# The first norms of an encoder trunk: x loaded ahead of the identity, operand parts written straight from PSUM, weights set behind the norms

## The chip, the cores and the metric

The kernel runs on one core of one Trainium2 chip. The core has TensorE (matrix products, into the accumulation memory PSUM with its 8 banks), VectorE, ScalarE (ACT), GpSimd (POOL) and SyncE (SP, which here only issues transfers), and 16 DMA engines that all transfers share. The metric is the device time of one execution in microseconds (us); of the kernel before there are three runs, 2758.95, 2759.03 and 2759.92 us, with the median 2759.03.

## The reference, cut to what matters

Two sequences, of 512 and 256 tokens of width 1024, go through the same two layers. A layer is: a gated feed-forward network (FFN), a token mixer, and a second FFN, each on normed input and added to x. Layer 0 mixes by a gated linear recurrence in both directions, layer 1 by windowed attention; a last norm closes the trunk. All is in 32-bit floats.

```python
def rmsnorm(x, g):
    y = xf * lax.rsqrt(jnp.mean(xf * xf, axis=-1, keepdims=True) + NORM_EPS)
    return (y * g.astype(F32)).astype(x.dtype)

def swiglu_ffn(x, w1, w2):                       # w1: 1024 x 5632, w2: 2816 x 1024
    gate, up = jnp.split(x @ w1, 2, axis=-1)
    return (jax.nn.silu(gate) * up) @ w2

for li in range(DEPTH):                          # DEPTH = 2
    x = x + 0.5 * swiglu_ffn(rmsnorm(x, norm_g[li, 0]), ffn_w1[li, 0], ffn_w2[li, 0])
    ...
```

## The kernel before

The 768 tokens of both sequences are six blocks of 128 rows; blocks 0 to 2 are half 0 and blocks 3 to 5 half 1, so a half has 384 columns once it is turned. x stays in on-chip memory (SBUF).

*Products.* A product of two 32-bit operands is made of three products of a faster, shorter format (fp32r): each operand is split into a high part, which is the operand rounded by a copy, and a low part, the operand less the high part. `mm3` gives high x high, high x low and low x high, where the weight is the first factor in `up_plain`: its low part is wanted by the third product, the low part of the activations by the second. ACT makes high parts and VectorE low parts.

*Start.* `setup` loads the identity (SP's queue) and the norm scales, lower bounds and head scales (ACT's queue), turns the latter on TensorE and copies them into `cols`. `load_x` issues, on SP, blocks 0 to 2 of x, the first two weight tiles, then blocks 3 to 5; later weights follow. At most four raw weight tiles are held, so the fifth waits until the first was split. `norm_block` squares and sums a block on ACT, takes the root on ACT, inverts it on VectorE and scales the block there. `turn(half, part, row)` turns four of the eight 128-column slices of a half on TensorE, three transposes to a bank; ACT copies each bank, times the norm's scale, into a plain block (`tn`), and `put` splits two slices at a time into operand parts: a cast on ACT and a subtraction on VectorE over 768 elements. Norms and turns of half 1 are put into a list (`later`), and `up_plain` takes one entry at set places between its products (`run_later`).

*FFN.* The first two column tiles of the gate and of the up half of `w1` are done by plain products (`up_plain`): for each half of the tokens four weight tiles, eight slices of 1024 each, three products a slice; 192 products of 384 columns in all. Its end for one tile is Silu on ACT and a multiplication on VectorE. The other 20 column tiles are done in pairs (`up_pair`, `product`, L423) by a scheme of seven block products in place of eight, which needs sums and differences of the four operand blocks: `sums` makes them on VectorE from the plain blocks `tn` and splits them (`t1`, `t4`, `t3`, `t2`, for two slices at a time). A pair takes its seven products in the order of `UP`: first `p1` with the block b00, then `p7` with `t3`. `down_quad` does the same for `w2`; ahead of its first group six additions and subtractions on VectorE (L483, L484) bring x into the form that the scheme wants.

*What sets the order.* The program is written in one order, and a planner sets each engine's order before the run from its own estimate of costs: an instruction that is ready by that estimate may go ahead of an earlier one that is not. So the six additions of L483 and L484 run on VectorE between 13 and 31 us, and the load of the sinks (L121) is ACT's first issue. `issue_after(ins)` holds what is traced in its block behind `ins`, on the engine of `ins` alone; it adds no wait. In the kernel before it keeps the loads in order and the first norms one behind the other.

## Time and profile before

| | |
|---|---|
| median of three runs | 2759.03 us |
| profiled execution, its own time | 2760.57 us |
| its span, from the first to the last instruction | 2758.8 us |
| mean granted clock of TensorE | 0.998 |
| TensorE products, busy | 2733.7 us (99%), 17281 |
| VectorE busy | 2100.5 us (76%) |
| ACT busy | 1327.5 us (48%) |
| POOL busy | 309.2 us (11%) |
| first product of `up_plain` | at 14.78 us |
| first product of L423 | at 54.80 us |

How to read the lines below. A line of the timeline has the start in us from the span's start, the time to the end of the last of the group, the engine, the line of the kernel, the operation, the tiles written and read with their shapes, and the number of instructions merged; in brackets stands the idle time of the engine just before and what ended it. SPq and ACTq are issues of transfers, PEld the load of the fixed operand of a product. Products overlap, so the time from one start to the next (the pitch) is shorter than one's duration; fp32r products appear as f32. A line of the table of windows has the window, its length, the busy time and the number of instructions of each engine asked for (all of them in the order TensorE, weight load, VectorE, ACT, POOL), the granted clock of TensorE as a share of full speed, the DMA engines' share and GB/s. A line of groups has the line, the engine, the operation, the tiles and shapes, the count, then the busy time in us and the mean of one in ns, then idle time before.

### The profile page before, as it was taken

How to read it: one execution, taken by the hardware profiler on the slowest of the kernel's cores; microseconds unless marked ns; L12 is line 12 of the kernel's file. 1: busy time of each engine (PE TensorE's matmuls, PEld its weight loads, DVE VectorE, ACT ScalarE, POOL GpSimd, SP SyncE). 2: the span in 40 equal slices, each digit the busy share in tenths (PEclk: the TensorE clock that was granted, in tenths of full speed). 3: DMA queues.
4: the chain of work that ended last, by engine and by line, in shares of the span. 5: the costliest groups of instructions: out<-in, count | busy, mean ns of one | idle time of the engine just before them, and what ended most of it. 6: DMA issues, size and time to landing. Idle time of an engine off the chain costs nothing.

```text
span 2758.8 us, 44483 instructions
## 1 busy us (share of the span) xinstructions
PE 2733.7 (99%) x17281; PEld 2481.9 (90%) x17281; DVE 2100.5 (76%) x3662; ACT 1327.5 (48%) x2479; POOL 309.2 (11%) x315
## 2 busy tenths in 40 slices
...
DMA packets 330117, 291.63 MB, mean 106 GB/s; under 512 B 11609, under 2 KB 257841, under 8 KB 329905
## 3 DMA queue, kind: packets, MB, share of 16 engines
...
## 4 chain that ended last, share of the span: by engine, by line
PE 95%; DVE 2%; ACT 2%; DMA 1%; issue 0%; DVEq 0%; SPq 0%; ACTq 0%
PE ps L423 41%; PE ps L498 20%; PE ps L263 9%; PE ps L265 9%; PE ps L264 9%; PE ps L694 1%; PE ps L1230 1%; PE ps L1169 1%; PE ps L839 1%; PE ps L1221 1%; PE ps L325 1%; DMA wr<-wr 1%; PE ps L815 0%; DVE x L520 0%; ACT big L328 0%
## 5 line engine op out<-in xcount | busy, mean ns | idle before, releaser
L423 PE MATMUL ps<-big,w 128*128 128x384 f32 x6720 | 1169.2, 334 | 0.0
L423 PEld LDWEIGHTS ps<-big,w 128*128 128x128 f32 x6720 | 1165.9, 188 | 1.6
L204 ACT CAST w<-wr 128x512 fp32r<-128x512 f32 x600 | 415.1, 706 | 707.4 <-DVE wr L218 371.6
L205 DVE TENSOR_TENSOR w<-wr,w 128x512 fp32r<-128x512 f32 (+1 forms) x520 | 448.5, 866 | 180.9 <-ACT w L204 176.0
L498 PE MATMUL ps<-w,big 128*128 128x512 f32 x2520 | 579.0, 390 | 2.0 <-DVE x L520 1.9
L498 PEld LDWEIGHTS ps<-w,big 128*128 128x128 f32 x2520 | 471.0, 188 | 104.8 <-ACT big L268 4.5
L520 DVE SCALAR_TENSOR_TENSOR x<-ps,x 128x512 f32<-128x512 f32 x468 | 303.6, 683 | 10.2 <-PE ps L265 10.0
L146 POOL DMA_DIRECT2D s<-wr x120 | 105.1, 875 | 1662.9 <-DMA wr<-in_ffn_w_dram 804.5
L263 PE MATMUL ps<-w,big 128*128 128x512 f32 x624 | 253.0, 405 | 0.3
L265 PE MATMUL ps<-w,big 128*128 128x512 f32 x624 | 244.8, 392 | 1.0 <-DVE big L332 1.0
L264 PE MATMUL ps<-w,big 128*128 128x512 f32 x624 | 244.8, 392 | 0.0
L268 ACT CAST big<-tA 128x384 fp32r<-128x384 f32 x296 | 148.1, 513 | 162.2 <-DVE tA L458 76.8
L263 PE MATMUL ps<-big,w 128*128 128x384 f32 (+2 forms) x640 | 219.2, 344 | 3.2 <-ACT big L268 1.9
L264 PE MATMUL ps<-big,w 128*128 128x384 f32 (+2 forms) x640 | 216.3, 338 | 0.7 <-DVE big L269 0.6
L265 PE MATMUL ps<-big,w 128*128 128x384 f32 (+2 forms) x640 | 215.5, 337 | 0.0
L269 DVE TENSOR_TENSOR big<-tA,big 128x384 fp32r<-128x384 f32 x296 | 183.9, 632 | 12.9 <-ACT big L268 12.0
L172 DVE TENSOR_TENSOR w<-wr,w 128x1024 fp32r<-128x1024 f32 x92 | 111.9, 1222 | 78.4 <-ACT w L171 72.6
L263 PEld LDWEIGHTS ps<-w,big 128*128 128x128 f32 x624 | 117.5, 188 | 29.3 <-issue 5.6
L205 POOL TENSOR_TENSOR w<-wr,w 128x512 fp32r<-128x512 f32 x80 | 123.3, 1541 | 179.7 <-ACT w L204 155.2
L171 ACT CAST w<-wr 128x1024 fp32r<-128x1024 f32 x92 | 96.5, 1052 | 97.3 <-PE ps L264 77.7
L265 PEld LDWEIGHTS ps<-w,big 128*128 128x128 f32 x624 | 117.4, 188 | 27.7 <-DVE big L332 1.7
L264 PEld LDWEIGHTS ps<-w,big 128*128 128x128 f32 x624 | 117.7, 189 | 21.8 <-issue 0.4
...
## 6 DMA issues: line engine op xcount, KB each, us to landing
wr<-in_ffn_w_dram SPq DMA_DIRECT2D x264, 512.0 KB, 3.9
...
```

Of the source, the lines that this page charges most:

```text
L146: self.nc.gpsimd.dma_start(out, src, accum_op=ALU.add)
L172: self.nc.vector.tensor_sub(lo, raw, hi.bitcast(F32))
L204: nc.scalar.copy(h, src)
L205: low = (eng or nc.vector).tensor_sub(l, src, h.bitcast(F32)).ins
L263: nc.tensor.matmul(out, a[0], b[0], start=first, stop=False)
L264: nc.tensor.matmul(out, a[0], b[1], start=False, stop=False)
L265: nc.tensor.matmul(out, a[1], b[0], start=False, stop=last)
L268: self.nc.scalar.copy(hi, src)
L269: self.nc.vector.tensor_sub(lo, src, hi.bitcast(F32))
L423: self.nc.tensor.matmul(ps, a[x], b[y], start=first and k == 0 and i == 0, stop=k == 3 and i == 2, skip_group_check=True,)
L498: nc.tensor.matmul(ps, a[x], w[y], start=name == chain and kp == 0 and q == 0, stop=kp == 1 and q == 2, skip_group_check=True,)
L520: self.nc.vector.scalar_tensor_tensor(x, ps, c, x, ALU.mult, ALU.add)
```

## The change

- `setup`: VectorE first clears a tile, and TensorE does 21 products of that tile with itself (128 x 128, into a bank that nobody reads). The identity is loaded from ACT's queue and not from SP's. The turning of the scales is put off into a function, `turn_cols`, whose copy stands behind the scaling of block 2 on VectorE.
- `norm_block`: block 1's square and sum run on VectorE (`tensor_tensor_reduce`).
- `turn(..., straight=True)` for half 0: from each bank ACT writes the high part and VectorE the low part of the operand; the plain blocks that `sums` needs are put together there, high plus low, by four additions of 768 elements.
- The first weight's subtraction is done in two halves of 512.
- Order: the first weight is staged between the two turns of half 0, the second after them; the norms of half 1 follow in `load_x` itself and no longer out of the list, the third weight behind the scaling of block 4 and the fourth behind that of block 5; the sinks' load stands behind the last root, Silu behind it too; the four additions in `sums` and the six of `down_quad` stand behind the scaling of block 5 or, once it is there, the last low part of b01. In the list two empty entries take the first two places, so that the turns of half 1 and the sums are taken one place later.

```diff
@@ -41,6 +41,7 @@
 RAWBUFS = 4
 SLOTS = 21
 RING = 1024
+WARM = 21
 UP = ("p1", "p7", "p2", "p5", "p4", "p6", "p3")
 DOWN = ("p1", "p2", "p5", "p4", "p7", "p6", "p3")
 FACTOR = {"p1": "b00", "p2": "b10", "p3": "b11", "p4": "t4", "p5": "t1", "p6": "t2", "p7": "t3"}
@@ -94,12 +95,17 @@
         nc, cp = self.nc, self.cp
         self.consts = consts
         ident, rows = consts[0], consts[4]
+        zero = self.tmp(TA)[:, :P]
+        nc.vector.memset(zero, 0.0)
         self.eps = cp.tile([P, 1], F32, name="eps")
         nc.vector.memset(self.eps, EPS)
+        idle = self.ps(P)
+        for _ in range(WARM):
+            nc.tensor.matmul(idle, zero, zero, start=True, stop=True)
+        raw = self.tmp(P)
+        nc.scalar.dma_start(raw, ident)
         warm = self.stat(1)
         nc.scalar.activation(warm, self.eps, AF.Sqrt)
-        raw = self.tmp(P)
-        nc.sync.dma_start(raw, ident)
         self.identr = cp.tile([P, P], F32R, name="ident_r")
         nc.vector.tensor_copy(self.identr, raw)
         self.ident = self.identr.bitcast(F32)
@@ -109,10 +115,14 @@
         for r in rows:
             nc.scalar.dma_start(cols[lo : lo + r.shape[0], :], r)
             lo += r.shape[0]
-        pt = self.ps(n)
-        nc.tensor.transpose(pt, cols[:n, :], self.ident[:n, :n])
         self.cols = cp.tile([P, n], F32, name="cols")
-        nc.vector.tensor_copy(self.cols, pt)
+
+        def turn():
+            pt = self.ps(n)
+            nc.tensor.transpose(pt, cols[:n, :], self.ident[:n, :n])
+            nc.vector.tensor_copy(self.cols, pt)
+
+        self.turn_cols = turn
 
     def load_tables(self):
         nc, cp = self.nc, self.cp
@@ -169,7 +179,10 @@
             n = shape[0] * shape[1]
             hi, lo = (self.wtile()[:, :n].rearrange("p (a b) -> p a b", a=shape[0]) for _ in range(2))
             self.nc.scalar.copy(hi, raw)
-            self.nc.vector.tensor_sub(lo, raw, hi.bitcast(F32))
+            some = shape[0] if self.staged else NC // 2
+            for k in range(0, shape[0], some):
+                ks = slice(k, k + some)
+                self.nc.vector.tensor_sub(lo[:, ks, :], raw[:, ks, :], hi[:, ks, :].bitcast(F32))
             self.staged[key] = (hi, lo, 2)
 
         return [(2, go)]
@@ -266,11 +279,12 @@
 
     def split(self, src, hi, lo):
         self.nc.scalar.copy(hi, src)
-        self.nc.vector.tensor_sub(lo, src, hi.bitcast(F32))
+        return self.nc.vector.tensor_sub(lo, src, hi.bitcast(F32)).ins
 
     def load_x(self, srcs):
         nc = self.nc
         self.x = [None] * NBLK
+        self.whole = []
         last = None
         blocks = [srcs[s][lo : lo + P, :] for s, (_, n) in enumerate(SEQS) for lo in range(0, n, P)]
         for b, src in enumerate(blocks):
@@ -285,31 +299,39 @@
         order = None
         for b in range(HB):
             with self.tc.issue_after(order) if order else nullcontext():
-                order = self.norm_block(b)
-        self.turn(0, 0, 0)
-        self.turn(0, 1, 0)
+                order = self.norm_block(b, b == 1)
+        with self.tc.issue_after(self.scaled):
+            self.turn_cols()
+        self.turn(0, 0, 0, True)
         with self.tc.issue_after(order):
             self.stage_next()
-            self.stage_next()
-        self.load_tables()
-
-        def rest():
-            for b in range(HB, NBLK):
-                self.norm_block(b)
-
-        self.later(rest, lambda: self.turn(1, 0, 0), lambda: self.turn(1, 1, 0), self.sums)
-
-    def norm_block(self, b):
+        self.turn(0, 1, 0, True)
+        self.stage_next()
+        for b in range(HB, NBLK):
+            with self.tc.issue_after(order):
+                order = self.norm_block(b)
+            if b > HB:
+                with self.tc.issue_after(self.scaled):
+                    self.stage_next()
+        self.normed, self.mixed = order, self.scaled
+        with self.tc.issue_after(order):
+            self.load_tables()
+        self.later(lambda: None, lambda: None, lambda: self.turn(1, 0, 0), lambda: self.turn(1, 1, 0), self.sums)
+
+    def norm_block(self, b, on_dve=False):
         nc = self.nc
         xn, r = self.big([P, D]), self.stat(1)
-        nc.scalar.activation(xn, self.x[b], AF.Square, accum_out=r)
+        if on_dve:
+            nc.vector.tensor_tensor_reduce(xn, self.x[b], self.x[b], 1.0, 0.0, ALU.mult, ALU.add, r)
+        else:
+            nc.scalar.activation(xn, self.x[b], AF.Square, accum_out=r)
         last = nc.scalar.activation(r, r, AF.Sqrt, bias=self.eps, scale=1.0 / D).ins
         nc.vector.reciprocal(r, r)
-        nc.vector.tensor_scalar(xn, self.x[b], r, None, ALU.mult)
+        self.scaled = nc.vector.tensor_scalar(xn, self.x[b], r, None, ALU.mult).ins
         self.xn[b] = xn
         return last
 
-    def turn(self, half, part, row):
+    def turn(self, half, part, row, straight=False):
         nc = self.nc
         feeds_ffn = row % 3 != 1
         if half == 0 and part == 0:
@@ -324,15 +346,28 @@
                 src = self.xn[HB * half + i][:, m * P : (m + 1) * P]
                 nc.tensor.transpose(pt[:, i * P : (i + 1) * P], src, self.ident)
             g = self.cols[:, row * NC + m : row * NC + m + 1]
-            if feeds_ffn:
+            if straight:
+                key = (f"b{part}{half}", m % 4 // 2)
+                if key not in self.ops:
+                    self.ops[key] = self.big([P, 2, 2, H], F32R)
+                hi, lo = (self.ops[key][:, m % 2, i, :] for i in range(2))
+            elif feeds_ffn:
                 nc.scalar.activation(self.block(part, half, m % 4), pt, AF.Copy, scale=g)
                 continue
-            hi, lo = (self.h[m][:, i, half * H : (half + 1) * H] for i in range(2))
+            else:
+                hi, lo = (self.h[m][:, i, half * H : (half + 1) * H] for i in range(2))
             nc.scalar.activation(hi, pt, AF.Copy, scale=g)
             nc.vector.scalar_tensor_tensor(lo, pt, g, hi.bitcast(F32), ALU.mult, ALU.subtract)
-        if feeds_ffn:
-            for kp in range(2):
-                self.put(f"b{part}{half}", kp, self.tn[(part, half)][:, kp])
+        for kp in range(2 if feeds_ffn else 0):
+            name = f"b{part}{half}"
+            if straight:
+                self.block(part, half, 0)
+                hi, lo = (self.ops[(name, kp)][:, :, i, :].bitcast(F32) for i in range(2))
+                self.whole.append((self.tn[(part, half)][:, kp], hi, lo))
+            else:
+                low = self.put(name, kp, self.tn[(part, half)][:, kp])
+                if self.mixed and part == 0:
+                    self.mixed = low
 
     def block(self, part, half, k):
         if (part, half) not in self.tn:
@@ -341,7 +376,7 @@
 
     def put(self, name, kp, src):
         t = self.ops[(name, kp)] = self.big([P, 2, 2, H], F32R)
-        self.split(src, t[:, :, 0, :], t[:, :, 1, :])
+        return self.split(src, t[:, :, 0, :], t[:, :, 1, :])
 
     def operand(self, name, k):
         t = self.ops[(name, k // 2)]
@@ -359,11 +394,16 @@
         put("t2", b11)
 
     def sums(self):
+        with self.tc.issue_after(self.mixed) if self.whole else nullcontext():
+            for parts in self.whole:
+                self.nc.vector.tensor_add(*parts)
+        self.whole = []
         for kp in range(2):
             tiles = (self.tn[(i // 2, i % 2)][:, kp] for i in range(4))
             self.mix(*tiles, lambda name, src: self.put(name, kp, src))
 
     xn = [None] * NBLK
+    normed = mixed = None
 
     def after_block(self, b, row):
         if row is None:
@@ -411,7 +451,9 @@
                 self.done((tag, j, c))
             pss.append(ps)
         t = self.tmp(H)
-        self.nc.scalar.activation(t, pss[0], AF.Silu)
+        with self.tc.issue_after(self.normed) if self.normed else nullcontext():
+            self.nc.scalar.activation(t, pss[0], AF.Silu)
+        self.normed = None
         self.nc.vector.tensor_mul(t, t, pss[1])
         return t
 
@@ -480,8 +522,10 @@
         if g == 0:
             for i in range(HB):
                 x12, x21, x22 = cols(HB + i, 0), cols(i, 1), cols(HB + i, 1)
-                nc.vector.tensor_add(x12, x12, x22)
-                nc.vector.tensor_sub(x21, x21, x22)
+                with self.tc.issue_after(self.mixed) if self.mixed else nullcontext():
+                    nc.vector.tensor_add(x12, x12, x22)
+                    nc.vector.tensor_sub(x21, x21, x22)
+            self.mixed = None
         banks = {}
         for name in DOWN:
             wh, wl = self.take((tag, "down", g, name))
```

## The prediction

> **What bounds the kernel now.** I read the page first, for the bound of the whole, then the timeline of the first 60 us, where everything in the change lies, then the table of windows for the clock and for VectorE's load.
>
> ```profile
> span 2758.8 us, 44483 instructions
> PE 2733.7 (99%) x17281; PEld 2481.9 (90%) x17281; DVE 2100.5 (76%) x3662; ACT 1327.5 (48%) x2479; POOL 309.2 (11%) x315
> ```
>
> TensorE is busy for 99% of the span, so at most some 25 us (2758.8 - 2733.7) can be had from idle time, and what is to be had at the start is the time until the stream of products runs without a stop. The timeline shows how that time goes:
>
> ```profile
> 0.74 0.38 SPq L102 DMA_DIRECT2D tB<-in_ident_dram  x1
> 1.18 1.37 SPq L279 DMA_DIRECT2D x<-in_x_prompt_dram  x3
> 5.57 1.06 ACT L305 ACTIVATE big<-x 128x1024 f32<-128x1024 f32 x1 [2.88 <-DMA x<-in_x_prompt_dram]
> 8.09 4.75 PE L325 MATMUL ps<-ident_r,big 128*128 128x128 f32 x24 [0.42 <-DVE big L308]
> 10.07 0.75 DVE L308 TENSOR_SCALAR big<-x,stat 128x1024 f32<-128x1024 f32 x1
> 10.15 1.05 ACT L171 CAST w<-wr 128x1024 fp32r<-128x1024 f32 x1 [0.31 <-DMA wr<-in_ffn_w_dram]
> 11.23 1.22 DVE L172 TENSOR_TENSOR w<-wr,w 128x1024 fp32r<-128x1024 f32 x1 [0.41 <-ACT w L171]
> 12.02 2.00 ACT L328 ACTIVATE big<-ps,cols 128x384 f32<-128x384 f32 x4 [0.82 <-PE ps L325]
> 13.88 1.58 ACT L268 CAST big<-big 128x768 fp32r<-128x768 f32 x2
> 14.76 1.83 DVE L269 TENSOR_TENSOR big<-big,big 128x768 fp32r<-128x768 f32 x2 [0.89 <-ACT big L268]
> 14.78 0.44 PE L263 MATMUL ps<-big,w 128*128 128x384 f32 x1 [1.95 <-ACT big L268]
> 15.78 0.69 PE L264 MATMUL ps<-big,w 128*128 128x384 f32 x1 [0.55 <-DVE big L269]
> ...
> 21.28 0.33 PE L263 MATMUL ps<-big,w 128*128 128x384 f32 x1
> 24.92 1.03 PE L325 MATMUL ps<-ident_r,big 128*128 128x128 f32 x8
> 26.14 0.34 PE L265 MATMUL ps<-big,w 128*128 128x384 f32 x1
> 26.57 1.98 ACT L171 CAST w<-wr 128x1024 fp32r<-128x1024 f32 x2
> 27.65 0.44 PE L263 MATMUL ps<-big,w 128*128 128x384 f32 x1 [1.17 <-ACT w L171]
> 27.92 2.35 DVE L172 TENSOR_TENSOR w<-wr,w 128x1024 fp32r<-128x1024 f32 x2
> 28.47 0.42 PE L264 MATMUL ps<-big,w 128*128 128x384 f32 x1
> 29.19 0.45 PE L265 MATMUL ps<-big,w 128*128 128x384 f32 x1
> ```
>
> The first of the 192 products of `up_plain` starts at 14.78, the second at 15.78. The first weight's 24 products end where the second weight's begin, at 21.28. The third weight is cast late (26.57), so TensorE waits at 27.65 and again for the low part at 29.19. After that nothing stops it until the pair products of L423:
>
> ```profile
> 54.80 5.36 PE L423 MATMUL ps<-big,w 128*128 128x384 f32 x30
> ```
>
> (5.36 - 0.33) / 29 = 0.173 us is the pitch of one product at full clock. 192 of them are 33.3 us, and the 24 transposes of the second half, at 0.109 (below), 2.6. So 54.80 less 35.9 leaves 18.9 us before and between, and the change can only cut there. Whatever moves 54.80 moves the end by as much, since no wait on a fixed time follows.
>
> The clock, in a part of the timeline and in three windows of 3.4 us:
>
> ```profile
> 9.00 2.98 PE L325 MATMUL ps<-ident_r,big 128*128 128x128 f32 x13
> 31.04 1.04 PE L325 MATMUL ps<-ident_r,big 128*128 128x128 f32 x8
> 8.60:12.04 3.44, 3.44 (x18) 3.44 (x17) 2.54 (x5) 2.28 (x5) 0.00 (x0) 1.00 1.15 325
> 12.04:15.45 3.41, 1.24 (x8) 0.74 (x6) 1.79 (x3) 3.41 (x7) 0.00 (x0) 1.00 1.02 389
> 15.45:18.87 3.42, 3.09 (x10) 3.10 (x11) 3.10 (x5) 3.42 (x8) 0.00 (x0) 0.50 1.17 292
> ```
>
> Transposes run at (2.98 - 0.42) / 12 = 0.213 us each up to 12.0 and at (1.04 - 0.28) / 7 = 0.109 later: the array was at half clock until about 12.04, though the granted column shows 1.00 there, with no record yet. A window with TensorE busy for 1.24 of 3.41 us was followed by one at 0.50.
>
> **The change part by part.** Times are in the profiled execution, whose own time is 2760.57 us (span 2758.8 and 1.8 around it); that is 1.54 above the median of the runs, 2759.03, and I carry the gain over to the median.
>
> *x first.* SP's first issue becomes block 0 of x at 0.74 and not 1.18: it lands at 5.57 - 0.44 = 5.13. The identity goes to ACT's queue ahead of the three row loads, where the load of the sinks stood, and is wanted only by the first transpose. Nothing is late for it.
>
> *Block 1's square on VectorE.* Its reduction has no row of 1024 elements; the nearest are
>
> ```profile
> L1185 DVE CUSTOM_DVE_ANT_0 big<-ps,big,nsinks 128x256 f32<-128x256 f32 x64 | 27.3, 480 | 3.4 <-PE ps L1169 3.3
> L1185 DVE CUSTOM_DVE_ANT_0 big<-ps,big,nsinks 128x384 f32<-128x384 f32 x32 | 17.8, 612 | 1.2 <-PE ps L1169 1.0 <-PE ps L265 0.2
> 5.20:8.60 3.40, 0.89 (x4) 0.69 (x5) 1.19 (x4) 2.96 (x7) 0.00 (x0) 1.00 1.04 381
> ```
>
> 132 ns for 128 elements give 0.612 + 5 x 0.132 = 1.27 us; L172's 1.22 is the other end; with the read of the sum I take 1.35. The DMA runs at 381 GB/s here, so block 1 lands 0.524 MB / 381 GB/s = 1.38 after block 0, at 6.5. The reduction holds VectorE until 7.9; queued behind it is block 0's reciprocal and scaling (ends 8.9, was 8.03), and ACT's square of block 2 stands behind block 1's root (8.2, was 8.37). Block 2's scaling then ends at about 10.85, as before (10.82). If block 0's scaling goes first, it is 11.8; if x lands sooner than I think, 10.4. The earlier x is spent here: zero.
>
> *Zeros.* 21 plain products of 128 columns. Such products stand in the recurrence:
>
> ```profile
> L815 PE MATMUL ps<-x,big 128*128 128x128 f32 x128 | 15.6, 275 | 0.0
> ```
>
> 15.6 / 128 = 0.12 us at full clock, 0.21 to 0.24 at half: they run from about 1.0 to 5.5 or 6.0, hidden under the wait for x, and end before the first transpose (8.9). The clock rises at the end of one busy window; three idle microseconds follow, which by the row 12.04:15.45 is enough to lose it, and the transposes raise it again, as they did at 12.04. So the first bank is full at 11.2 with the array warm throughout, or at 8.9 + 16 x 0.213 + 0.42 + 0.2 = 12.9 with it cold; I take 12.3, against 12.02 now. What the zeros do gain is that no window stays empty just before the products. The Trainium skill (TensorE: Matmul & The Clock Gate, Part 4: PE-mode transpose) has it that transposes don't count as work for the gate; by that the products would start at half clock, which is a rival below. The trace disagrees: the pitch went from 0.213 to 0.109 in a stretch that held only transposes.
>
> *Parts straight from banks.* The scaled copy, two casts and two subtractions go; each bank gives a high part (ACT) and a low part (VectorE). The later norms have this very pair:
>
> ```profile
> L331 ACT ACTIVATE big<-ps,cols 128x384 fp32r<-128x384 f32 x32 | 16.4, 583 | 11.4 <-PE ps L325 9.2 <-DMA spill<-x 2.1
> 510.78 1.67 DVE L332 SCALAR_TENSOR_TENSOR big<-ps,cols,big 128x384 fp32r<-128x384 f32 x3
> ```
>
> The first product needs one bank only: 12.3 + 0.58 + 0.07 = 12.95 (was 14.78), the second after 0.61 more, 13.6 (was 15.78). From there a bank costs 3 x 0.173 = 0.52 on TensorE, (1.67 - 0.61) / 2 = 0.53 on VectorE and (2.00 - 0.59) / 3 = 0.47 on ACT. The first weight's first half of low parts (0.6) is done in the wait for the banks; its second half may stand between the banks (+0.6) or not. The eighth low part is done at 13.6 + 7 x 0.53 = 17.3 to 17.9, and the first weight ends at 17.7 to 18.3: 18.0, against 21.28. In the old figure 1.4 us is the half clock: ten products at 0.32.
>
> *Other weights behind the norms.* The second weight's low part follows the eighth bank on VectorE, 17.9 + 1.15 = 19.0; its third product waits for that (wanted at 18.35). It ends at 19.0 + 22 x 0.173 = 22.8, or 22.2 without that stall. The third weight: ACT has eight banks to 12.3 + 8 x 0.47 = 16.1, the second weight 17.15, norms of blocks 3 and 4 at 1.47 each 20.1, then its cast, 21.15; low part 22.4, wanted at 23.15. The 1.66 us lost between 26.31 and 29.36 in the old timeline (3.05, less three products and eight transposes) go. If ACT does block 5's norm first, 0.75 come back. Both extra table loads of ACT (Silu, Sqrt, Silu) shrink to one; they lay beside the products.
>
> Then 144 products and 24 transposes: 22.8 + 24.97 + 2.62 = 50.4 against 54.80. **The sum is 4.4 us**: 3.3 at the first weight, -0.6 at the second, 1.7 at the third. With warm transposes, the half early and no stall it is 6.6; with the cold start and the late cast 3.0.
>
> *What is late next: VectorE's sums.* `sums` must give `t3` before the second product of pair 2, 12 products after 54.80 (56.9 now), its second half by 57.9.
>
> ```profile
> 50.91 2.69 DVE L269 TENSOR_TENSOR big<-big,big 128x768 fp32r<-128x768 f32 x3
> 5.57:53.60 48.03, 38.96 (x53) 0.96 0.64 176
> L269 DVE TENSOR_TENSOR big<-big,big 128x768 fp32r<-128x768 f32 x16 | 14.5, 954 | 3.0 <-ACT big L268 3.0
> L484 DVE TENSOR_TENSOR x<-x,x 128x512 f32<-128x512 f32 x3 | 2.0, 687 | 0.7 <-DMA x<-in_x_prompt_dram 0.7
> ```
>
> The sums end at 53.6 now, with 9.07 us idle on VectorE before. The change adds to it 1.35 (the square), 8 x 0.61 - 4 x 0.954 = 1.06 (low parts), 4 x 0.954 = 3.8 (the four adds that put the plain blocks together), 0.14 (the halved subtraction): 6.4 us. The six x-adds of `down_quad` (6 x 0.687 = 4.1) now stand behind the low part of b01, about 29.5. VectorE starts at 6.5. With no idle time the sums would end at 6.5 + 38.96 + 6.4 = 51.9 with the x-adds ahead of them and 47.8 with these behind; they are wanted at 50.4 + 2.1 = 52.5. I reckon 4 to 5 us idle (waiting for banks, and for b01 at 25 to 28): they are just in time with the x-adds behind, since these rank later in the program. Cost: 0; at worst, the x-adds ahead, 3.5.
>
> *A half-clock window later.*
>
> ```profile
> 2080.52:2083.93 3.41, 3.41 (x13) 3.02 (x12) 1.42 (x9) 2.29 (x8) 0.00 (x0) 0.50 0.40 132
> ```
>
> Here 3.4 us pass at half clock in the attention. Where windows fall against the work shifts with the start; this can vanish or come twice, 1.7 us either way.
>
> **The rivals.**
>
> *Clock.* The zeros' window is lost, the transposes don't raise the clock, and the first products run at half: 0.6 for the late bank (12.9), and over one window of 3.4 us a bank's three products take 0.96 (row 15.45:18.87; ten in 3.2) and not 0.53, 1.5 us. Gain 4.4 - 2.1 = 2.3: 2756.7. For it: the rule above, three idle microseconds after the zeros. Against: the rise at 12.04.
>
> *VectorE becomes the bound at the sums.* Pair 2's second product waits up to 3.5 us: gain 0.9, 2758.1. For it: 81% busy up to 53.6 (38.96 of 48.03), and 6.4 more in less time. Against: the x-adds are last in rank.
>
> *Slower: VectorE keeps its idle time.* The same place, but none of the 9.07 us is used up, since each low part waits for a bank and each sum for a cast of ACT. The sums end at 53.6 + 6.4 = 60.0, the second half of `t3` is wanted at 57.9 by the old timeline: 2.1 us slower, 2761.1. It decides from sums that end after 57.9; over 0.2% slower needs 63.4. Against: the x-adds and the wait for the eighth bank are taken out of exactly this time.
>
> *The change doesn't do what it says at the third weight.* The planner sets ACT's order; if all three norms and Silu's table load go ahead of the cast (its order is tied to VectorE's scaling only), the wait of 1.7 us stays: gain 2.7, 2756.3.
>
> **How the numbers follow.** 0.2% of 2759.03 is 5.5 us, about what a measurement of this kernel can tell from no change. My forecast is 2759.03 - 4.4 = 2754.6: faster by 0.16%, by that bound no change. Chances: forecast, with its own gain of 3.0 to 6.6 (2752.4 to 2756.0), 0.58, of which 0.18 lies beyond 5.5; more than that, with the window at 2080 gone too, 0.07; clock 0.12; VectorE's bound 0.12; third weight 0.06; slower 0.05, of which 0.02 over 5.5. Faster 0.18 + 0.07 = 0.25, slower 0.02, same 0.73. The range from 2752.3 to 2758.3 holds all but the 0.07, the 0.05 and some 0.06 at its ends.
>
> **What would show it.** In the profile after: SP's first issue of x at 0.74; block 2's scaling ending near 10.85; a group of 21 plain products from 1 us on; transposes of the first half at 0.213 or 0.109; the first product near 13.0 and the second near 13.6; the second weight from 18.0; no idle time of TensorE on L171's cast; L423 from 50.4; the last 768-wide L269 of VectorE before 52.5. L423 later than 53 with no wait on the sums would make steps at the start wrong; L423 near 50 and a time above 2757 would make the sums, or something after 60 us that I hold to shift whole, the place of the loss.

## The result

The changed kernel takes 2752.6 us (median of 10 runs, 2751.7 to 2753.4), the kernel before beside it 2759.15: 6.55 us less, a ratio of 0.9975 with a 95% interval of 0.9966 to 0.9985. The forecast was 2754.6, "by that bound no change"; the time lies inside its range of 2752.3 to 2758.3, and beyond its bound of 5.5 us for no change. The direction held, and so did the mechanism at the start. The size is the sum of three errors that partly cancel, and a part of one lies 1200 us behind the change.

The page of the kernel after (its profiled execution took 2752.51 us), first the span, then the busy time of each engine:

```profile
span 2750.7 us, 44570 instructions
PE 2734.1 (99%) x17323; PEld 2483.8 (90%) x17323; DVE 2101.2 (76%) x3674; ACT 1323.8 (48%) x2471; POOL 313.1 (11%) x315
```

TensorE is as busy as before, and the span is 8.1 us shorter. The start, in the timeline (L104 zeros, L327 and L325 squares, L330 scalings, L347 first transposes, L181 and L185 the first weight's cast and low part, L359 and L360 the parts straight from banks, L276 to L278 the products that were L263 to L265):

```profile
1.06 6.38 PE L104 MATMUL ps<-tA 128*128 128x128 f32 x42 [1.06 <-DVE eps L101]
4.60 1.06 ACT L327 ACTIVATE big<-x 128x1024 f32<-128x1024 f32 x1 [1.91 <-DMA x<-in_x_prompt_dram]
6.00 1.23 DVE L325 CUSTOM_DVE_ANT_0 big<-x 128x1024 f32<-128x1024 f32 x1 [0.98 <-DMA x<-in_x_prompt_dram]
8.15 3.30 PE L347 MATMUL ps<-ident_r,big 128*128 128x128 f32 x24 [0.54 <-DVE big L330]
9.33 0.75 DVE L330 TENSOR_SCALAR big<-x,stat 128x1024 f32<-128x1024 f32 x1
10.51 3.89 ACT L359 ACTIVATE big<-ps,cols 128x384 fp32r<-128x384 f32 x8
11.12 2.19 DVE L360 SCALAR_TENSOR_TENSOR big<-ps,cols,big 128x384 fp32r<-128x384 f32 x4
11.79 0.44 PE L276 MATMUL ps<-big,w 128*128 128x384 f32 x1 [0.34 <-DVE big L360]
12.08 0.34 PE L277 MATMUL ps<-big,w 128*128 128x384 f32 x1
14.50 0.45 PE L277 MATMUL ps<-big,w 128*128 128x384 f32 x1 [0.17 <-DVE big L360]
15.93 1.22 DVE L185 TENSOR_TENSOR w<-wr,w 128x1024 fp32r<-128x1024 f32 x1
21.13 0.33 PE L276 MATMUL ps<-big,w 128*128 128x384 f32 x1
48.75 11.43 PE L465 MATMUL ps<-big,w 128*128 128x384 f32 x65
```

The first product stands at 11.79 (14.78 before), the third weight's first at 21.13 (27.65) and L465, the old L423, at 48.75 (54.80): a lead of 6.05 us. Then TensorE and VectorE, further down the timeline:

```profile
49.22 2.69 DVE L282 TENSOR_TENSOR big<-big,big 128x768 fp32r<-128x768 f32 x3
63.27 15.72 PE L465 MATMUL ps<-big,w 128*128 128x384 f32 x89 [0.66 <-DVE tA L494]
85.37 3.01 PE L542 MATMUL ps<-w,big 128*128 128x512 f32 x12 [1.58 <-DVE x L564]
```

TensorE now waits twice for VectorE, 0.66 and 1.58 us, where it waited for nothing before. For what follows I number TensorE's product records, transposes among them, in order of time from 0, without the zeros, so that one number is the same work in both kernels. At number 500 (104.69 us before, 101.36 after) the lead is down to 3.3 us. And yet 6.55 us arrive at the end. So the document has two questions: which part makes the lead at 48.75, and where the other 3 us come from.

### The profile page after: what moved, and what is told of

It reads as the page before. It is cut to its first block, busy times and chain, and to the rows that moved or that the text cites. A ratio compares the mean times of both kernels' runs of the same rounds, so it can differ in the third digit from the quotient of the medians.

```text
span 2750.7 us, 44570 instructions
## 1 busy us (share of the span) xinstructions
PE 2734.1 (99%) x17323; PEld 2483.8 (90%) x17323; DVE 2101.2 (76%) x3674; ACT 1323.8 (48%) x2471; POOL 313.1 (11%) x315
## 4 chain that ended last, share of the span: by engine, by line
PE 94%; DVE 4%; ACT 2%; issue 0%; DMA 0%; SPq 0%; DVEq 0%; ACTq 0%
PE ps L465 41%; PE ps L542 21%; PE ps L276 9%; PE ps L278 8%; PE ps L277 8%; PE ps L738 1%; PE ps L1274 1%; PE ps L1213 1%; PE ps L883 1%; PE ps L1265 1%; DVE big L282 1%; PE ps L347 0%; PE ps L859 0%; DVE w L218 0%; DVE x L564 0%
## 5 line engine op out<-in xcount | busy, mean ns | idle before, releaser
L465 PE MATMUL ps<-big,w 128*128 128x384 f32 x6720 | 1169.6, 334 | 0.7 <-DVE tA L494 0.7
L465 PEld LDWEIGHTS ps<-big,w 128*128 128x128 f32 x6720 | 1165.9, 188 | 2.7 <-DVE tA L494 1.0
L542 PEld LDWEIGHTS ps<-w,big 128*128 128x128 f32 x2520 | 471.7, 188 | 102.6 <-DVE x L564 3.6
L564 DVE SCALAR_TENSOR_TENSOR x<-ps,x 128x512 f32<-128x512 f32 x468 | 304.1, 686 | 10.1 <-PE ps L278 9.9
L276 PE MATMUL ps<-w,big 128*128 128x512 f32 x624 | 252.5, 405 | 0.3
L278 PE MATMUL ps<-w,big 128*128 128x512 f32 x624 | 244.6, 392 | 1.0 <-DVE big L360 1.0
L276 PE MATMUL ps<-big,w 128*128 128x384 f32 (+2 forms) x640 | 218.7, 343 | 0.5 <-DVE big L360 0.3
L278 PE MATMUL ps<-big,w 128*128 128x384 f32 (+2 forms) x640 | 214.8, 336 | 0.0
L185 DVE TENSOR_TENSOR w<-wr,w 128x1024 fp32r<-128x1024 f32 (+1 forms) x93 | 112.2, 1211 | 77.3 <-ACT w L181 71.4
L276 PEld LDWEIGHTS ps<-w,big 128*128 128x128 f32 x624 | 117.2, 188 | 29.4 <-issue 5.6
L181 ACT CAST w<-wr 128x1024 fp32r<-128x1024 f32 x92 | 96.7, 1054 | 96.2 <-PE ps L277 77.6
L278 PEld LDWEIGHTS ps<-w,big 128*128 128x128 f32 x624 | 117.1, 188 | 27.5 <-DVE big L360 1.7
L156 POOL DMA_DIRECT2D wr<-wr x100 | 87.7, 877 | 460.1 <-ACT w L217 153.7
```

What stands on the lines that cost most here:

```text
L156: self.nc.gpsimd.dma_start(out, src, accum_op=ALU.add)
L185: self.nc.vector.tensor_sub(lo[:, ks, :], raw[:, ks, :], hi[:, ks, :].bitcast(F32))
L276: nc.tensor.matmul(out, a[0], b[0], start=first, stop=False)
L278: nc.tensor.matmul(out, a[1], b[0], start=False, stop=last)
L465: self.nc.tensor.matmul(ps, a[x], b[y], start=first and k == 0 and i == 0, stop=k == 3 and i == 2, skip_group_check=True,)
L542: nc.tensor.matmul(ps, a[x], w[y], start=name == chain and kp == 0 and q == 0, stop=kp == 1 and q == 2, skip_group_check=True,)
```

## The experiments

The table has for each kernel the median, how much it is faster than the kernel before in the same set of runs, the interval of the ratio, and from its profile the times of L465 (L423 before; the line number differs in some kernels) and of product 500. The column "behind" is the time from product 500 to 13,500 and from 14,000 to 17,270 together. What lies between 13,500 and 14,000 is left out: there a half-clock window costs 1.1 to 1.6 us in some executions and nothing in others, in both kernels (77.7 to 79.3 us for the stretch).

| kernel | median | gain | ratio | L465 | no. 500 | behind |
|---|---|---|---|---|---|---|
| before (its profile) | 2759.15 | | | 54.80 | 104.69 | 2564.2 |
| e5 before, again | 2758.97 | 0.3 | 0.999-1.0009 | 55.11 | 104.98 | 2563.7 |
| after (its profile) | 2752.60 | 6.55 | 0.9966-0.9985 | 48.75 | 101.36 | 2561.1 |
| e1 after, again | 2752.50 | 6.8 | 0.9966-0.9985 | 48.68 | 103.11 | 2561.2 |
| f4 after, again | 2752.78 | 6.9 | 0.9965-0.9984 | 48.70 | 101.24 | 2559.9 |
| f6 after, again | 2752.19 | 7.2 | 0.9963-0.9984 | 48.57 | 101.16 | 2561.5 |
| e2 no zeros | 2756.79 | 2.5 | 0.998-0.9998 | 49.59 | 102.09 | 2565.0 |
| e6 zeros alone | 2755.77 | 3.5 | 0.9977-0.9996 | 54.40 | 104.31 | 2560.8 |
| e7 10 zeros | 2753.75 | 5.5 | 0.997-0.9988 | 50.01 | 102.61 | 2561.2 |
| e8 not straight | 2754.48 | 4.8 | 0.9972-0.999 | 51.62 | 102.60 | 2560.9 |
| f3 half straight | 2754.47 | 5.2 | 0.9973-0.9991 | 49.79 | 102.67 | 2562.1 |
| e11 norms later | 2755.05 | 4.5 | 0.9973-0.9991 | 48.79 | 101.78 | 2561.8 |
| e12 identity on SyncE | 2753.23 | 6.3 | 0.9971-0.9989 | 49.64 | 102.26 | 2560.1 |
| f1 first weight whole | 2751.93 | 7.8 | 0.9963-0.9984 | 48.56 | 101.25 | 2560.4 |
| f2 square on ScalarE | 2752.78 | 6.9 | 0.9966-0.9984 | 48.61 | 101.37 | 2560.3 |
| f5 both of these | 2752.80 | 6.6 | 0.9966-0.9984 | 48.76 | 101.40 | 2560.8 |
| e4 sums twice | 2753.29 | 6.0 | 0.9968-0.9986 | 48.61 | 101.58 | 2560.7 |
| e3 additions on GpSimd | 2762.14 | -2.85 | 1.0001-1.0018 | 54.89 | 110.39 | 2560.4 |
| e10 32 narrow zeros | 2762.39 | -2.9 | 1.0003-1.0021 | 56.43 | 109.33 | 2561.4 |
| e9 64 narrow zeros | 2777.22 | -17.7 | 1.0051-1.0077 | 69.72 | 122.31 | 2563.4 |

### Chance, or the change: e1, e5, f4, f6

Nothing is edited in these four.

> The changed kernel once more, nothing edited, for a second profile and a second interval. Theory (the start is worth 6.05 us, and VectorE's backlog gives 2.8 of it back by 90 us): the clock is at full before the first transposes, the pair products (L465) start at 48.75 +- 0.2 us, TensorE waits 0.5 to 1.2 us for VectorE's L494 near 63 and 1.5 to 2.2 us for L564 near 84, and the median stays 5.5 to 7.5 us under the kernel before. Rival (the gain beyond 100 us in the first pair of profiles, among it a half-clock window of the attention that is missing after, belongs to the change): the profile again shows no half-clock window before the tail.

> The kernel before, unedited: a second profile of it beside its own time. The lead of the changed kernel at product 500 (some 100 us) was 3.3 us in the first pair of profiles, while its median gain is 6.6. Theory A (the rest of the gain hangs on the start: the first 55 us set at which phase the weights' loads, sums and casts meet the products later): this profile loses again 0.5 us in the products from number 884 (about 175 us, down products waiting for VectorE) and 1.2 to 1.5 us from number 9188 (about 1249 us), at the same places as in the first profile. Theory B (single waits that come and go by chance, in either kernel): the losses lie at other places. Both: L423 begins at 54.8 within 0.3, time 2759 within 1.5.

> The changed kernel, unedited, once more. Its median was 2752.6 and 2752.5 in two sets of runs. Expected 2752.5 within 0.6, L465 at 48.7, waits of 0.6 for L494 and 1.6 to 1.8 for L564, nothing over 0.1 us lost from product 9188; half-clock windows, if any, cost 1.4 to 1.8 us each where they fall on the stream.

> The changed kernel, unedited, beside the simpler one: 2752.6 within 0.6, L465 at 48.7.

The changed kernel comes back at 2752.2 to 2752.8, the kernel before at 2758.97, so the gain is no accident of one set. L465 comes within 0.2 us of 48.7 in each profile; it is the sharpest readout here. e1's number 500 is 1.75 us late because that one execution had TensorE at half clock from 86.17 to 89.58 us. The half-clock window near 2080 us, which the first pair of profiles showed only before, shows in e1 and f4 too and is absent in e5: it is chance, and it explains why that pair differs by 8.1 us and the medians by 6.55.

e5 answered its own question plainly. The kernel before loses time at the same place as in its first profile, in the products from number 9188, some 1250 us in. The waits of TensorE around that place in e5 (us in total, times, longest):

```profile
PE ps L498 <- DVE x L520: 1.3, 1, 1.3
```

The first profile of before has 1.17 us here (its row stands below), the four profiles of the changed kernel nothing. So this is no chance; it must be something that the change shifts and that stays shifted.

### The zeros: e2, e6, e7

```diff
e2:  the tile of zeros, the idle bank and the 21 products are left out
e6:  before.py with only these added
e7:  -WARM = 21
     +WARM = 10
```

> The changed kernel without the 21 products of zeros and the clearing of their tile. Theory (the zeros hold the array at full clock through the transposes and the first products): transposes of half 0 run at 0.213 us each, the first bank is full near 11.8 and not 10.4, the first weight's products run in part at 0.32 us each; L465 starts 1.5 to 3 us later than 48.75. Rival (my prediction: the transposes raise the clock by themselves, the zeros only fill a window): L465 within 0.6 us of 48.75, no difference in time.

> The kernel before, with the 21 products of zeros alone added ahead of the identity's turn; the order of loads, norms, copies and weights is that of before. Nothing is left out. Theory (the zeros bridge to the first transposes and keep the array at full clock; they don't move x or the weights): first transpose at 8.1, last of the first 24 at about 11.3 in place of 12.56, no half-clock window at 15.45, so that the 24 products of the first weight lose their 0.42 to 0.69 pitch only where the low parts are late; first product 13.7 to 14.2 (14.78), L423 at 53.0 (52.2 to 53.9). Median if the later gain follows the start: 2756 to 2757; if it follows the zeros themselves: 2754 to 2755. Rival (the first products are set by ScalarE's copies and the cast, not by the transposes): first product 14.6 or later, L423 at 54.3 or later, median 2758 to 2759.

> The changed kernel with 10 products of zeros in place of 21: at 0.427 us a product at half clock and 0.213 at full they end near 4.7 us, 3.4 us ahead of the first transposes at 8.15. Theory A (the zeros must run on until the transposes begin, an idle gap of 3 us costs the clock): the first 24 transposes run at half clock again for most of their time, end near 12.5 to 13.3, the first product comes at 12.8 to 13.4 and L465 at 49.3 to 49.6, as with none. Theory B (that the clock was raised once is enough, it is taken back only after a longer idle time): transposes end by 11.4, L465 at 48.7, time as the changed kernel's.

First the clock. The transposes and the first products of e2, of e7 and of e6 in the timeline:

```profile
8.45 5.12 PE L342 MATMUL ps<-ident_r,big 128*128 128x128 f32 x24 [0.99 <-DVE big L325]
13.33 0.42 PE L271 MATMUL ps<-big,w 128*128 128x384 f32 x1
13.59 0.34 PE L272 MATMUL ps<-big,w 128*128 128x384 f32 x1
```

```profile
1.06 3.87 PE L104 MATMUL ps<-tA 128*128 128x128 f32 x20 [1.06 <-DVE eps L101]
8.25 5.38 PE L347 MATMUL ps<-ident_r,big 128*128 128x128 f32 x24 [0.34 <-DVE big L330]
13.29 0.67 PE L276 MATMUL ps<-big,w 128*128 128x384 f32 x1
```

```profile
14.52 0.64 PE L269 MATMUL ps<-big,w 128*128 128x384 f32 x1 [2.04 <-ACT big L274]
27.38 0.44 PE L269 MATMUL ps<-big,w 128*128 128x384 f32 x1 [1.30 <-ACT w L177]
```

A product of zeros is two records; 42 fill the time from 1.06 to 7.44, at a pitch of 0.213 us a record up to about 4.0 and 0.112 behind. They end 0.7 us ahead of the transposes, which then take 3.30 us. With 20 records they end at 4.93, TensorE has next to nothing for 3.3 us, the clock falls back (the trace has it at half from 7.38 to 14.20), and the transposes take 5.38 us. With none they take 5.12. So theory A of e7 holds: the zeros must bridge, raising the clock once is not enough. Their worth at L465 is 0.9 us (49.59 against 48.7); ten of them are worse than none (50.01), since e7's first products are still slow (0.67) where e2's run at full clock.

e6 shows the reverse: with warm transposes but the old copies and casts, the first product still waits 2.04 us for ACT's cast, and the third weight 1.30. L465 gains 0.4. My rival for e6 was right about the start (54.3 or later), and its median of 2758 to 2759 was wrong: e6 is 3.5 us faster. e2 is as odd the other way: 5.2 us of lead at L465 and only 2.5 at the end. Both oddities stand in the column "behind": 2565.0 without zeros, 2560.8 with them.

### What zeros change 1200 us later: e9, e10

The profiles record TensorE's instruction fetches as a queue of their own, 16 KB a time: 135 on the page of before. 17,281 products and as many weight loads are 34,562 instructions, 256 to a fetch, that is a fetch in 128 products. The Trainium skill (Runtime: NRT & Kernel Launch, Instruction fetch mechanics) states the 16 KiB block and its 256 instructions, and this count agrees. 42 records more with their weight loads are 84 instructions: each later fetch comes some 40 products earlier in the stream. The place ahead of product 9188, from POOL's issue of a weight's accumulating transfer on, in the timelines of before and of after:

```profile
1239.34 0.89 POOL L146 DMA_DIRECT2D wr<-wr  x1 [11.01 <-ACT w L204]
1245.51 2.00 ACT L204 CAST w<-wr 128x1024 fp32r<-128x1024 f32 x2 [5.51 <-DMA wr<-wr]
1247.64 4.28 PE L498 MATMUL ps<-w,big 128*128 128x512 f32 x18
1253.09 3.23 PE L498 MATMUL ps<-w,big 128*128 128x512 f32 x13 [1.17 <-DVE x L520]
```

```profile
1235.16 0.89 POOL L156 DMA_DIRECT2D wr<-wr  x1 [10.97 <-ACT w L217]
1239.91 1.05 ACT L217 CAST w<-wr 128x1024 fp32r<-128x1024 f32 x1 [3.92 <-DMA wr<-wr]
...
1243.64 6.55 PE L542 MATMUL ps<-w,big 128*128 128x512 f32 x28
```

The same transfer is issued 8.3 and 8.5 us ahead of the down products, and ACT's cast of what it brings follows the issue after 6.2 us and after 4.75. It is late by 1.4 us, VectorE's low part behind it, then `add_x`, and TensorE waits 1.17 us for a bank. The transfers in this place, in the 13 us that end 2 us ahead of product 9188: the fetch (packets, MB, share of the engines), where there is one, and the accumulating transfer with its time to landing, for before, after and e9:

```profile
q8 instruction: 1, 0.02, 0.7%
...
wr<-wr POOLq DMA_DIRECT2D x1, 512.0 KB, 5.7
```

```profile
wr<-wr POOLq DMA_DIRECT2D x1, 512.0 KB, 4.6
```

```profile
q8 instruction: 1, 0.02, 0.5%
...
wr<-wr POOLq DMA_DIRECT2D x1, 512.0 KB, 5.9
```

e9 and e10 move the fetches by the count of instructions alone. 128 records are a whole period, which puts the fetches back where they were before the change; 64 are half of one.

```diff
-WARM = 21
+WARM = 64          # e10: 32, and 84 columns
-            nc.tensor.matmul(idle, zero, zero, start=True, stop=True)
+            nc.tensor.matmul(idle[:, :43], zero, zero[:, :43], start=True, stop=True)
```

> The changed kernel with 64 products of zeros of 43 columns in place of 21 of 128: 128 matmul records in place of 42, at about the same time in all (2752 columns against 2688). Nothing is left out. In the profiles TensorE's instructions are fetched 16 KB at a time, once in some 128 products; the zeros of the changed kernel shift each fetch by about 40 products against the product stream (at product 9188 the last fetch before it came at product 9131 without zeros, 9096 with 21, 9114 with 10). 128 records shift it by a whole period, to where it lay in the kernel before. Theory (a fetch that falls into the transfer of a weight delays it, the cast, and a sum on VectorE behind it): the waits of the kernel before return at the same products: 1.1 to 1.6 us from 9188, 0.3 to 2.6 from 884, 0.2 to 0.7 from 15536, and the one of 0.3 to 1.0 from 9644 goes; from product 500 to the end the stream takes 2 to 3.5 us longer than in the changed kernel, so that with L465 at 48.7 to 49.3 the median is 2755 to 2756.5. Rival (what later waits there are follows the start time or chance, not the count of instructions): no more than 0.3 us from 9188, and the median stays with the start, 2752.5 to 2753.3.

> As the run before it, with 32 products of zeros of 84 columns: 64 records, the fetches shifted by half a period against the kernel before. Theory of the fetches: the places where the stream waits after product 500 are again others than with 42 records (neither 1.1 us from 9188 nor the same set as in the changed kernel), and the sum of them differs by up to 2 us either way; median 2751 to 2755. Rival: same places and the time of the changed kernel, 2752.5 within 0.7.

I meant to keep the start as it was, and failed: both medians missed by far, because narrow products are not cheaper. The zeros of e9:

```profile
1.05 27.54 PE L104 MATMUL ps<-tA 128*128 128x43 f32 x128 [1.05 <-DVE eps L101]
```

27.54 us for 128 records, and 13.95 for the 64 of e10: each takes 0.2135 us, with 43 or 84 columns as with 128 at half clock, and the clock does not rise, in 13.95 us with 84 columns or in 27 with 43: the transposes behind them start at 0.213. That costs the start 21 and 8 us and leaves the count of products untouched, so the question is still answered product by product. Fetches fall at these product numbers ahead of 9188, with the landing of the transfer (its packets run from product 9131 to 9147, or to 9155 where it is late) and the time lost between 9100 and 9200 against the best profile:

| kernels | fetch at product | landing, us | lost, us |
|---|---|---|---|
| before, e5, e2, e9 | 9131, 9135, 9132, 9137 | 5.7, 6.0, 5.8, 5.9 | 1.4, 1.6, 1.1, 1.2 |
| e7 (20 records) | 9114 | 4.6 | 0.0 |
| after, f4, and 12 others with 42 records | 9093 to 9096 | 4.6 | 0.0 to 0.1 |
| e10 (64 records) | 9079 | 4.6 | 0.0 |

(The landings are those of before, e5, e2, e9, e7, after, f4 and e10.) A kernel whose fetch falls into the transfer loses, whatever its start: e9 starts 13 us later than any other and loses, e2 starts within 0.9 us of the changed kernel and loses, e6 starts with the kernel before and does not. None of the others does. In the packets of all twenty profiles it is the same: the 512 KB accumulating transfers with less than 20 KB of other traffic beside them take 2.77 us from the first packet to the last (median of 365; nine in ten at most 2.80) where no fetch falls in, and 3.25 (median of 34; the longest 4.34) where one does. The whole stretch "behind" says the same: 2563.4 to 2565.0 us for these four, mean 2564.1, and 2559.9 to 2562.1 for all fourteen profiles with 42 records, mean 2560.9; 20 and 64 records have 2561.2 and 2561.4. That is **3.2 us** for the count of instructions. Three places account for 2.1 of it, in which each of the four loses and none of the fourteen does: 1.3 from 9188, 0.5 between 16,900 and 17,000 and 0.25 between 2200 and 2300; product by product, only the one at 9188 was followed back to its transfer. From 884 and from 15,536, which I named as well, profiles with 42 records lose up to 0.8 too, so there the fetch is one cause among others, and the largest single loss is 2.7 us from 884 in e2. e9 alone, with 2563.4, is 2.5 us over the mean of the fourteen. That section of the Trainium skill calls the cost of crossing a block mostly hidden; here no wait of TensorE in the profiles is put down to a fetch, but the weight's transfer takes longer.

The two parts add up. A profile's lead at number 500 over the mean of before and e5 (104.84), plus 2564.1 less its "behind", gives the gain in the median within 1.1 us for all kernels but e1 with its odd window: 3.5 + 3.0 = 6.5 for the changed kernel (measured 6.55), 2.75 - 0.9 = 1.9 for e2 (2.5), 0.5 + 3.3 = 3.8 for e6 (3.5), -17.5 + 0.7 = -16.8 for e9 (-17.7), -5.55 + 3.7 = -1.8 for e3 (-2.85).

### The parts from banks and the third weight: e8, f3, e11

```diff
e8:  -        self.turn(0, 0, 0, True)
     +        self.turn(0, 0, 0)
     -        self.turn(0, 1, 0, True)          # f3: this one alone
     +        self.turn(0, 1, 0)
e11: the loop over blocks 3 to 5 out of load_x and into the list:
     -        self.later(lambda: None, lambda: None, lambda: self.turn(1, 0, 0), ...)
     +        self.later(rest, lambda: None, lambda: self.turn(1, 0, 0), ...)
```

> The changed kernel with its parts of the first half made by plain copies out of the banks and a cast of both, as before, in place of the two parts straight from the banks; the adds of the whole parts fall away with it. My theory of the first weight (copies at 10.5 to 14.4, then casts of 0.79 for two blocks): first product at 13.0 to 13.5 (11.79 in the changed kernel), L465 at 49.4 to 50.3; VectorE, which is spared 8 subtractions of 0.55 and 4 adds of about 1.0 but gets four of 0.95, loses less at 62 (L465 for L494 0 to 0.4 in place of 0.7). Median 2753.5 to 2754.5. Rival (the first product may come later, since VectorE's backlog behind it takes back what is gained): first product as late, but the end within 0.7 of the changed kernel's, 2752 to 2753.2.

> The changed kernel with only the first part of the first half straight from its banks; the second part is made by plain copies and a cast, as before, and needs no whole sum behind. VectorE is spared two sums of about 1.0 and 4 subtractions of 0.55, and does two of 0.95 for them. Theory (the second part's casts come behind four copies, ScalarE sets the products from the 13th): first product at 11.8, a wait of 1 to 2 us at the 13th and 14th, L465 at 49.7 to 50.8; waits at 58 to 86 us smaller by 0.5 to 1.0, product 500 (101.4 in the changed kernel) at 101.4 to 102.5; median 2752.5 to 2754. Rival (the first part alone bridges the casts; VectorE's load decides): L465 at 48.7 to 49.2 and product 500 at 100.3 to 101.2, median 2751 to 2752.3.

> The changed kernel with the norms of the second half again in the list of later work, called with the first products, as before; zeros, x first, straight parts and the split first weight stay. My prediction put 1.7 us of the gain on the third weight, cast before the norms rather than behind them. Theory: the first two weights' products as in the changed kernel (first product 11.8, 25th 16.9, 49th 21.1), then again a wait for the third weight's cast and low part of 1 to 2 us; L465 at 49.8 to 50.8. Rival (TensorE comes to the third weight 5 us earlier than I reckoned the cast to be blocked; the cast waits for its transfer, not for the norms): 49th at 21.1, no wait, L465 within 0.3 of 48.7.

The first two products of e8, then the thirteenth and what follows it in f3 (whose first stands at 11.61):

```profile
13.16 0.44 PE L276 MATMUL ps<-big,w 128*128 128x384 f32 x1 [1.82 <-ACT big L281]
14.15 0.60 PE L277 MATMUL ps<-big,w 128*128 128x384 f32 x1 [0.55 <-DVE big L282]
```

```profile
14.98 0.44 PE L276 MATMUL ps<-big,w 128*128 128x384 f32 x1 [1.01 <-ACT big L281]
15.97 0.44 PE L277 MATMUL ps<-big,w 128*128 128x384 f32 x1 [0.55 <-DVE big L282]
```

Straight parts are worth 2.9 us at L465 (51.62 against 48.75, more than the 0.7 to 1.6 I expected), 1.0 of it with the second part (f3). At number 500 e8 lags by 1.2 us only: it has no wait for L494 at all, and waits 0.6 for L564 where the changed kernel waits 1.58. Those waits take back more than half of what the straight parts gain; what causes them is asked below. With one part straight, f3 is 1.8 us ahead of e8 at L465, and level with it at number 500 and in the median (2754.47 and 2754.48).

e11 hit its rival: the 49th product, the first of the third weight, comes at 21.17 and L465 at 48.79. The later norms may stay in the list, since ACT, spared four casts, is free for them from 15.2 us where it was 19.6 before. No single edit owns the 1.7 us of the third weight: with the casts back (e8) the order does it, with the order back (e11) the missing casts do. e11's median is 2.5 us over the changed kernel's, though; its profile shows 0.4 us of that by number 500 and 0.6 "behind". The rest cannot lie in that profile, whose execution took 2753.59, 1.5 us less than e11's median; where it is stays open.

### The small parts: e12, f1, f2, f5

```diff
e12: -        nc.scalar.dma_start(raw, ident)
     +        nc.sync.dma_start(raw, ident)
f1:  -            some = shape[0] if self.staged else NC // 2
     +            some = shape[0]
f2:  -                order = self.norm_block(b, b == 1)
     +                order = self.norm_block(b)
f5:  both edits of f1 and f2
```

> The changed kernel with the load of the identity back on SyncE ahead of x, as before. Theory (the place of the identity in SyncE's queue sets when x lands): block 0 at 5.0 to 5.6 in place of 4.60, first scaling, last first-half transpose and first product 0.4 to 1.0 later (first product 12.2 to 12.8), L465 at 49.1 to 49.8. Rival (the first scaled block waits for the reciprocal and the table of functions, not x; or the loads share the same engines either way): first product within 0.2 of 11.8, L465 within 0.2 of 48.7.

> The changed kernel with the low part of the first weight made in one subtraction (1.22 us) in place of two of 0.69. Theory (the split lets the parts' subtractions between its halves, and so the first product, come earlier): the first part's low subtraction ends 0.5 later, first product at 12.2 to 12.4 (11.79), and the second half of the weight is then ready earlier, so that L465 is at 48.75 to 49.2. Rival (the split only shifts work on VectorE, whose first ready low part of x sets the first product): first product within 0.15 of 11.79 and L465 within 0.15 of 48.75. Median in both 2752.5 to 2753.5, which can't tell them apart.

> The changed kernel with block 1's square again on ScalarE (1.06 us and its read of the sum) in place of VectorE's 1.23. Theory (ScalarE's three squares in a row set the norms): block 2's square starts 0.3 to 1.0 later than 7.83, its scaling ends at 10.5 to 11.2 (10.08), first product at 12.2 to 12.9, L465 at 49.1 to 49.9. Rival (block 2's landing near 7.8 sets its square either way): block 2's scaling within 0.2 of 10.08, L465 within 0.2 of 48.75.

> The changed kernel with both the first weight's low part in one subtraction and block 1's square on ScalarE. Alone they moved L465 from 48.7 to 48.56 and 48.61. Theory (both are off the path): L465 at 48.3 to 48.7, product 500 at 101.0 to 101.5, median 2751.5 to 2752.8, not to be told from the changed kernel's. Rival (together they meet: with the square on ScalarE the first weight's cast or the first low part comes later, and the whole subtraction then stands ahead of it): first product after 12.3, L465 after 48.9.

x first is worth 0.9 us at L465 (48.75 to 49.64) and at number 500, as the theory had it: in e12 ACT's first square starts later and the first product comes at 12.68.

```profile
5.28 1.06 ACT L327 ACTIVATE big<-x 128x1024 f32<-128x1024 f32 x1 [2.59 <-DMA x<-in_x_prompt_dram]
```

The split of the first weight and the square on VectorE are worth nothing: without the one L465 is at 48.56, without the other at 48.61, and both theories of mine fell. f1's first product is 0.3 later (12.05), but the 25th 0.1 earlier (16.78), because the weight's second half no longer stands between the banks. f2 scales block 2 by 9.94, 0.14 earlier than with the square on VectorE (10.08): block 0's reciprocal need not wait behind the square. f1's median is the lowest of all, 0.85 us under the changed kernel in the same set (f4), but of 7 runs only; without both parts (f5) it is 2752.8, beside 2752.2 for the changed kernel: not to be told apart, and no better. No version clearly beats the changed kernel.

### VectorE's load and the two waits: e4, e3

```diff
e4:  -                self.nc.vector.tensor_add(*parts)
     +                for _ in range(2):
     +                    self.nc.vector.tensor_add(*parts)
e3:  the six additions and subtractions of down_quad from nc.vector to nc.gpsimd,
     issued behind the fourth accumulating transfer
```

e4 does the four additions of the whole parts twice; what they compute is the same.

> The changed kernel with each of the four additions that put the plain blocks together done twice, to the same result: 3.5 to 3.8 us more for VectorE before the sums, nothing else. Theory (VectorE is the bound between 30 and 90 us, so every microsecond there is paid): TensorE's waits before 90 us grow from 2.7 to between 5 and 6.5 us in total; time 2.5 to 3.8 us longer than the changed kernel, near 2756. Rival (there is slack, the two waits come from the order of VectorE's instructions and not from its load): the waits grow by less than 1 us.

> The changed kernel with the six additions and subtractions that bring x into the form for the first down_quad on GpSimd, behind its fourth accumulating transfer (near 30 us), and not on VectorE: 4.1 us less for VectorE before 75 us. Theory (the 2.8 us that are given back between 60 and 90 us are VectorE's backlog): both waits of TensorE, on L494 near 63 and on L564 near 84, go or shrink to under 0.5 us together, and the time is 2 to 2.8 us under the changed kernel, near 2750. Rival (the weights' accumulating transfers on GpSimd's queue are what is late): the waits stay or grow, since GpSimd has 9 us more to do; time the same or longer by up to 2 us.

Twice the additions, 3.5 us more for a VectorE that has no idle time at all from 48.75 to 60 us in the changed kernel:

```profile
48.75:60.00 11.25, 11.25 (x66) 11.25 (x66) 11.25 (x19) 7.54 (x15) 1.12 (x2) 1.00 0.27 76
```

It costs 0.2 us at number 500 and 0.7 in the median; the theory, that every microsecond of VectorE is paid there, fell, and the rival was right. The waits of e4 between 40 and 90 us are moved, not longer:

```profile
PE ps L543 <- DVE x L565: 1.2, 1, 1.2
PE ps L466 <- DVE w L218: 0.7, 1, 0.7
```

So the waits do not grow one for one with VectorE's load. What stands ahead of the second one, in the timelines of before and of after:

```profile
75.63 0.85 POOL L146 DMA_DIRECT2D wr<-wr  x1 [8.37 <-DVE tA L468]
80.25 1.05 ACT L204 CAST w<-wr 128x1024 fp32r<-128x1024 f32 x1 [3.98 <-DMA wr<-wr]
83.92 4.28 PE L498 MATMUL ps<-w,big 128*128 128x512 f32 x18
```

```profile
75.23 0.86 POOL L156 DMA_DIRECT2D wr<-wr  x1 [8.96 <-DVE tA L494]
78.83 4.96 PE L542 MATMUL ps<-w,big 128*128 128x512 f32 x21
79.86 2.00 ACT L217 CAST w<-wr 128x1024 fp32r<-128x1024 f32 x2 [6.96 <-DMA wr<-wr]
```

The accumulating transfer of a weight is issued at nearly the same time in both, ACT's cast follows 0.4 us apart, and behind it come VectorE's low part and `add_x`; TensorE arrives at its down products 5.1 us sooner. From this pair alone one would say that the chain has a time of its own and that the lead runs into it. e9, whose L465 comes at 69.72, shows that this is not so:

```profile
84.22 15.72 PE L465 MATMUL ps<-big,w 128*128 128x384 f32 x89 [0.64 <-DVE tA L494]
96.17 0.85 POOL L156 DMA_DIRECT2D wr<-wr  x1 [9.26 <-DVE tA L494]
106.31 3.92 PE L542 MATMUL ps<-w,big 128*128 128x512 f32 x16 [1.56 <-DVE x L564]
```

Both waits are as long as in the changed kernel, and they end 14.50 and 36.59 us behind L465 (14.52 and 36.62 there); the transfer is issued 26.45 us behind it (26.48), where the kernel before has 20.83. So a start that is 21 us later takes the whole chain with it, and the loss comes with the changed program, not with the lead. The table says the same. From L465 to number 500 it is 49.9 us in before, e5 and e6, 51.0 in e8, and 52.5 to 53.0 in all others but e1, with its half-clock window in this stretch, and e3 (below). The issue of the transfer waits for VectorE (L494, L468 before), and VectorE has more to do here than before: the parts from banks, the four additions that put them together, and three of the six additions and subtractions of `down_quad`, which all ran ahead of 31 us before and now start at 55.03, 57.31 and 70.97. e8, without the first two, loses 1.1 us in place of 2.7. What the moved operations and the order on VectorE cost of the rest, no run shows.

e3 was to free VectorE and did the opposite. VectorE and GpSimd from 30 us:

```profile
30.07 9.57 DVE L282 TENSOR_TENSOR big<-big,big 128x768 fp32r<-128x768 f32 x2 [0.66 <-ACT big L281]
30.19 1.65 POOL L528 TENSOR_TENSOR x<-x 128x512 f32<-128x512 f32 x1
...
36.38 1.56 POOL L529 TENSOR_TENSOR x<-x,x 128x512 f32<-128x512 f32 x1
```

Two subtractions of 0.95 us last 9.57 together, with GpSimd's six operations beside them from 30.19 to 37.94, and L465 goes to 54.89. Neither the theory nor the rival had this, and so e3 does not show what the six operations cost on VectorE. The Trainium skill (SBUF — State Buffer, SBUF: two separate sides) has it that VectorE operations with two SBUF inputs and GpSimd's hold a shared pair of ports one at a time, the other being blocked; this row agrees with it.

## Why the prediction was right and wrong, step by step

- **"Whatever moves 54.80 moves the end by as much, since no wait on a fixed time follows."** This is the step that failed, though not by a wait on a fixed time: a start that is moved by itself does move what follows by as much (against the changed kernel, e9 is 21.0 us later at L465 and 20.95 at number 500, e7 1.26 and 1.25, e12 0.9 and 0.9). But the change does more than move 54.80. It gives VectorE more work behind it, on which TensorE waits twice: 6.05 us of lead become 3.3 at product 500. And it shifts the fetches, which moves the end by 3.2 us more. The first stood in the prediction as "Cost: 0" (below), the second neither in the sum nor in a rival.
- **The sum, 4.4 us at L423.** It measured 6.05, inside its own bounds of 3.0 to 6.6. The first weight's term was mis-sized most: 3.3 reckoned, 4.4 measured (24 products are through at 16.90, where 18.0 stood). x lands at 4.60, not 5.13; block 2's scaling ends at 10.08, not 10.85; the first product comes at 11.79, not 12.95, the second at 12.08, not 13.6.
- **Zeros, "0.12 us each at full clock, 0.21 to 0.24 at half", "they end before the first transpose", with three idle microseconds behind.** The duration was read from a row that counts records as if each were a product; a product is two records, 0.30 us here on the mean, and the 21 of them reach to 7.44. With 10 (e7) the step's story of a lost clock comes true word for word. The mechanism was right, the size decided against it.
- **The clock rival.** The prediction already set the row of 12.04 against it. e9 settles it: after 27 us of narrow zeros at half clock, the plain transposes alone bring the pitch from 0.213 to 0.109 after twelve of them, and e2's first products, behind transposes only, run at full clock (0.34). By the rule of the Trainium skill (TensorE: Matmul & The Clock Gate, Part 4: PE-mode transpose) they would have run at half; these two runs disagree with it.
- **Second weight, -0.6 for a stall on its low part.** No stall: that low part ran from 15.93 to 17.15, ahead of its use, since the banks were done sooner.
- **Third weight, 1.7.** The wait went, as forecast; e11 shows that the reason given, the order of the norms, was not needed for it.
- **Block 1's square on VectorE, "zero".** Right: without it L465 is the same (f2). That it holds up block 0's reciprocal was foreseen; block 2's scaling ends 0.14 later for it.
- **Sums in time for `t3`, "Cost: 0".** Right for `t3`: the sums end at 51.9 (I had 52.5 as the bound), and pair 2 does not wait. Wrong as a cost: VectorE was full from there on, and TensorE waits for it 11 us later (0.66) and again at 85.37 (1.58), which comes to 2.7 us by number 500. e8 shows 1.6 of it to be the straight parts'. Three of the six x-adds, moreover, went ahead of the sums (28.60 to 30.4) and not behind.
- **The rivals.** VectorE as the bound did not come at the sums, but 11 us behind them, and the slower case not at all; the half-clock window in the attention was correctly held to be chance.

In numbers: 4.4 forecast, 1.65 more at L465, 2.7 lost on VectorE by product 500, 3.2 from the fetches make 6.55. That the forecast missed by 2.15 us and not by more is luck: the two terms that it lacked nearly cancel.
